# Queue order of the weight sums in the first 58 steps, another ring for one factor of the rotation table, and moved slots in a hybrid decoder layer

## The chip, the cores and the metric

The kernel runs on one core of one Trainium2 chip. The metric is the device time of one execution in microseconds (us): 2327.57 us is the median of three runs (2327.4 to 2328.82). The profile shows one further execution of the same program.

## The reference, cut to what matters

One decoder layer for 512 tokens of width 2048, in float32:

```python
h = rms_norm(x, g_mix)
aq, ak, av, rq, rk, rv, rg = split(h @ w_in)          # 7 parts of 1024 columns
# 8 attention heads: QK-RMSNorm, rotation, block-sparse causal softmax attention
# 8 retention heads: rotation, decayed q k^T v in chunks, per-head RMS norm, silu(rg) gate
x = x + concat(a_out, r_out) @ w_o                    # w_o 2048 x 2048
h2 = rms_norm(x, g_ffn)
x = x + (silu(h2 @ w_gate) * (h2 @ w_up)) @ w_down    # 5632 wide
gate = sigmoid(rms_norm(x, g_ple) @ w_ple_gate + b_ple_gate)
x = x + (p @ w_ple_proj) * gate
```

The rotation multiplies with tables of cosines and sines. The retention heads use a transposed table `ropeT` of 128 x 2 x 512 values; in this kernel it is first multiplied by the inverse norm of each token's row, because `h` here is only scaled by the gain and not yet by the norm.

## The kernel before, in words

**Products.** Every float32 operand is split in a high and a low part (`split`, L51: ScalarE copies the high part, `wh` for weights; VectorE subtracts it from the source, which gives the low part `wl`). A product is three matmuls (`mm3`, L72): high with high, high with low, low with high. The large products use a Strassen-like scheme: of 2 x 2 blocks seven products are made, named "1", "5", "6", "3", "7", "2", "4" in this order. "5", "6", "7" and "4" need a sum of two weight blocks. VectorE makes it in place (`Group.add`, L317, which calls `plus` at L83, shown as `raw<-raw`), and then the sum is split.

**Steps.** `run` (L173) works through a list of steps, each one product name with one unit of 256 rows of weights. In iteration `i` it first calls `before(i)`, then adds for step i+3, extracts (splits) for step i+2 and multiplies for step i. In the iterations named by `close` the add is for step i+2. The loop only writes the program order. A planner then orders each engine's instructions by priority and by the times that it reckons with, so an instruction can run earlier than where it stands. `tc.issue_after(ins)` binds the instructions in its block to stand behind `ins` in the queue of that engine. Matmuls keep the program order (`in_order`). A group of four units has 28 steps. The last call of `run` (L1395) has 2 groups of the output product (`w_ow`), 11 of gate and up, 6 of down and 2 of the last gate; its adds are bound only behind `last_p`, which is the last multiplication of the last retention head.

**The stage between.** From about 350 to 700 us attention and retention are interleaved with five projections of `h` (`projection`, L781). Each projection has 32 slots of six matmuls into four banks `acc`. `at_slot(n, fn)` puts a piece of other work into slot n, `tick` (L735) runs it. The tables `V_AT`, `T3`, `ATTEND`, `RETAIN` and `MIXED` (L1136 to L1145) hold the slots: turning q and k (`turned`), scores, turning the softmax weights (`weights_turned`), the head's result, and `mixed`, which splits two heads' results into the seven factors of the output product. `in_place` (L909) rotates an attention block, `qk_ret` (L1005) takes a retention projection from its banks: ScalarE copies the halves crosswise (`mr`, L1015 and L1016), VectorE multiplies the bank by the table (`zr`, L1017), and only then is the bank free for the next projection; later `turned` (L1019) multiplies `mr` by the other half of the table and adds it.

**Rings.** Tiles of one tag share a few buffers. The ring "A" has two; a head's result stays in it until `mixed` has read it. The ring "rm" has four; `m`, `sq`, `mr` and some outputs of `mixed` use it. `tp` has two banks for transposes.

**The table.** `load_ropeT` (L838) stands in slot 58: a DMA of the table, four transposes that spread the inverse norm over the partitions, a ScalarE copy of these to `bc` (in ring "A"), and a VectorE product.

**The banks of the output product.** `multiply` (L352) of the first group, for product "1", takes four banks in one go, in the order X0, Z0, Z1, X1; they take the places of the four `acc` banks, whose last content (`pp`) ScalarE copies out at L1212. `take_over` (L1224) runs the last 16 slots inside the first eight iterations of the last `run`.

Of the kernel before, what the change touches and what calls it, by code (L numbers as in the profile page):

```python
# [33 lines left out]
def layer_kernel(ctx, tc, x, xT, pT, g_mix, wqk, w_vg, qk_norm, g_ret, w_ow, g_ffn,  # L34
# [135 lines left out]
    def later(n, fn):  # L170
        due.setdefault(now[0] + n, []).append(fn)

    def run(before=lambda i: None, behind=False, close=()):  # L173


        i = -3
        parts = {}
        while i < len(steps) or due:
            now[0] = i
            before(i)  # L180
            todo = [(2, "extract"), (3, "add"), (0, "multiply")]
            if i in close:
                todo = [(2, "add"), (2, "extract"), (0, "multiply")]
                if i + 1 not in close:
                    todo[2:2] = [(3, "add")]
            for n, act in todo:
                if 0 <= i + n < len(steps):
                    g, p, u = steps[i + n]
                    with ExitStack() as queued:
                        if act == "add" and (not behind or i < 8) and i not in close and parts.get(i + 1):  # L190
                            queued.enter_context(tc.issue_after(parts[i + 1][1].ins))
                        if act == "add" and last_p:
                            queued.enter_context(tc.issue_after(last_p[-1].ins))
                        made = getattr(g, act)(p, u)
                    if act == "extract":
                        parts[i + n] = made
                        splits.append(made)
            with ExitStack() as queued:
                for ins in parts.pop(i + 1, ()) if behind else ():
                    queued.enter_context(tc.issue_after(ins.ins))  # L200
                for fn in due.pop(i, []):
                    fn()
            i += 1
        steps.clear()

    def ev_tile(tag, bufs=2, shape=(P, T), name=None, dt=F32):
        return pools["ev"].tile(list(shape), dt, name=name or tag, tag=tag, bufs=bufs)
# [77 lines left out]
    class Group:  # L285
# [66 lines left out]
        def multiply(self, p, u):  # L352
            wh, wl = self.w.pop((p, u))
            k = BANK[p]
            first = p in OPENS and self.left[p] == len(self.units)
            if first:
                def bank(k, b):
                    return pools.get("chain" + k, pools["chain"]).tile([P, T], F32, name=k + str(b), tag=k + str(b))
                if self.spread and p == "1":
                    x = bank("X", 0)  # L360
                    self.bank["Z"] = [bank("Z", 0), bank("Z", 1)]
                    self.bank["X"] = [x, bank("X", 1)]
                elif not (self.spread and p == "5"):
                    self.bank[k] = [bank(k, b) for b in range(2)]
            self.left[p] -= 1
            last = self.left[p] == 0
            self.w[u] = wh, wl
            whole, lo, hi = (0, T), (0, T // 2), (T // 2, T)
            todo = [(0, u, whole), (1, u, whole)]
            if self.ends and p == "4":  # L370
                todo = [(0, u, whole)]
                if first:
                    self.bank["H"] = pools["chain"].tile([P, T], F32, name="Z1", tag="Z1")
                for c in (lo, hi) if self.left[p] != 1 else ():
                    todo += [(1, v, c) for v in ((u - 1, u) if last else (u,))]
            in_order[0] = in_order[0] or self.ends and p == "4"
            for b, v, (c0, c1) in todo:
                at = slice(b * P, (b + 1) * P)
                to = self.bank["H"] if c0 else self.bank[k][b]
                for c in range(2):  # L380
                    s = self.tiles[p].pair(2 * v + c)
                    mm3(to[:, :c1 - c0], s[:, 0, at], s[:, 1, at], *(x[:, c, c0:c1] for x in self.w[v]),
                        first and c == 0, last and v == u and c == 1, p in "237")
            if last:
                self.after(p)
                self.evac(self, p)
# [344 lines left out]
    def at_slot(n, fn):  # L731
        assert n > slot[0]
        pieces.setdefault(n, []).append(fn)
# [104 lines left out]
    def load_ropeT():  # L838
        t = ap.tile([P, 2, T], F32, name="ropeT", tag="rope")
        nc.sync.dma_start(t, ropeT_c)  # L840
        bc = ev_tile("A", name="bc")
        nc.scalar.activation(bc, over_partitions(rstd1), AF.Copy)
        nc.vector.tensor_tensor(t, t, bc[:, None, :].to_broadcast([P, 2, T]), op=ALU.mult)
        tables.append(t)
# [78 lines left out]
    def qk_attn(i):  # L923

        made, norms = [], []
        if i == 0:
            for b in range(NB):
                with tc.issue_after(splits[b - 5][1].ins):
                    in_place(0, b, made, norms)
        elif i < NPAIR - 1:  # L930
            for b in range(NB):
                at_slot((2 + b, 15 + b)[i - 1], lambda b=b: load_block(i, b, lead[0]))
                at_slot(((7, 11, 17, 20), (24, 30, 33, 36))[i - 1][b], lambda b=b: in_place(i, b, made, norms))
        else:
            zs = []
            for acc in projection(True):
                zs.append(rp_tile("z"))
                nc.scalar.activation(zs[-1], acc, AF.Copy)
            blocks[i] = zs
            for b in range(NB):  # L940
                def go(b=b):
                    known.setdefault(i, {})[b] = ms = stat.tile([P, 4], F32, name="ms", tag="rsqk", bufs=NB)
                    with behind_weights():
                        squares_of(zs[b], ms, b, rm_tile("sq"))
                    in_place(i, b, made, norms)
                at_slot(T3[b], go)
        return made, norms
# [57 lines left out]
    def qk_ret(i):  # L1005
# [25 lines left out]
                made[f] = parted(got[f][0])  # L1031
        for f, (z, m) in enumerate(got):
            if i < 2 * NPAIR - 1:
                at_slot(slot[0] + (6 + 2 * f if i < 2 * NPAIR - 2 else 7 + f), lambda z=z, m=m: turned(z, m))
                made.append(z)
        return made

# [87 lines left out]
    def mixed(i, made):  # L1125
# [3 lines left out]
        with ExitStack() as queued:  # L1129
            for ins in lead if i < 2 * NPAIR - 1 else ():  # L1130
# [1 line left out]
            factors(*made, lambda p: (direct if p in s_o else spilled)(p))  # L1132

    four = lambda n, m=None: (n, n + 1, *((n + 4, n + 5) if m is None else (m, m + 1)))
    V_AT = (3, 31, 55, 82, 108, 124, 145, 162)
    T3 = (48, 50, 52, 56)  # L1136
    ATTEND = (((4, four(7, 10), (11, 12, 14, 15), 20), (12, four(16, 21), four(21), 30)),
              ((23, four(26, 31), four(31, 38), 44), (34, four(39, 45), four(45), 53)),
              ((48, four(53), four(57), 70), (59, four(63, 73), four(72, 77), 81)),
              ((75, four(79), four(83), 92), (85, four(89), four(93, 103), 107)))  # L1140
    RETAIN = (((104, 103, 108, 114, 118, 121), (112, 105, 116, 122, 126, 128)),
# [3 lines left out]
    MIXED = (37, 67, 83, 109, 139, 152, 170, 192)  # L1145

    def heads(i, made):

# [9 lines left out]
        if i < NPAIR:  # L1158
            for j, (turns, steps_s, steps_w, last) in enumerate(ATTEND[i]):
                turned, scores, weights_turned, result = attend(*made, v, j)  # L1160
                put(turned, turns, turns + 1)
                put(weights_turned, *steps_w)
                put(scores, *steps_s)
                end(last, result)
        else:
            for j, (first, at, step_s, step_n, step_x, last) in enumerate(RETAIN[i - NPAIR]):
                begin, load, load_gate, scores, normed, scaled, result = retain(made, v, j, 2 * (i - NPAIR) + j)
                if (i, j) == (2 * NPAIR - 1, 1):
                    plan.append((170, load_gate))
                plan.extend(((first, begin), (at, load), (step_x, scaled)))  # L1170
                put(scores, *range(step_s, step_s + NB))
                put(normed, step_n, step_n + 1)
                end(last, result)
        for n, fn in plan:
            at_slot(n, fn)
# [2 lines left out]
    at_slot(2, lambda: nc.scalar.activation(stat.tile([P, 1], F32, name="sm"), neghalf, AF.Exp))  # L1178
    for i in range(2 * NPAIR):
        if i == NPAIR:  # L1180
            at_slot(58, load_ropeT)
        qk = qk_attn(i) if i < NPAIR else qk_ret(i)
        heads(i, qk)
    assert not gu_moves
# [207 lines left out]
        if i == b_at:  # L1392
            load_bias()

    run(before, True, range(-3, 10))  # L1395


def _constants():
# [68 lines left out]
```

## Time and profile before

| what | value |
|---|---|
| median of three runs | 2327.57 us |
| the profiled execution: its own time | 2327.24 us |
| its span (first to last instruction) | 2325.2 us |
| TensorE matmul busy | 2292.1 us, 99% |
| VectorE busy | 1917.9 us, 82% |
| ScalarE busy | 1243.3 us, 53% |
| GpSimd busy | 103.6 us, 4% |
| mean granted TensorE clock | 0.996 |

The execution's own time is 2.0 us more than its span, and 0.3 us less than the median. In the rows, PE is the TensorE's matmuls, PEld its weight loads, DVE is VectorE, ACT ScalarE, POOL GpSimd and SPq the queue that issues most DMAs. A time in square brackets behind a row is the engine's idle time just before it, with the instruction that ended it.

### The profile page before, as it was taken

The page shows a single profiled execution, that of the slowest core. Times are in us where ns is not written, and L with a number is a line of the kernel's source. Part 1 is how long each engine was busy: PE and PEld are TensorE (multiplying, and loading weights), DVE is VectorE, ACT ScalarE, POOL GpSimd, SP SyncE. Part 2 cuts the span into 40 slices and gives each one's busy share as a digit, 9 for nine tenths or more (in the row PEclk, how much of TensorE's full clock was granted, in tenths as well). Part 3 has the DMA queues.
Part 4 walks back from the last instruction along what each step waited for, and adds up shares of the span by engine and source line. Part 5 has one row for each costly group of instructions (what it writes and reads, how often), then busy time and mean ns, then how long its engine had stood idle before and what let it go on. Part 6 is the DMA issues. An engine that isn't in the chain of part 4 may idle for free.

```text
span 2325.2 us, 29619 instructions
## 1 busy us (share of the span) xinstructions
PE 2292.1 (99%) x10445; PEld 1893.7 (81%) x10445; DVE 1917.9 (82%) x2569; ACT 1243.3 (53%) x1975; POOL 103.6 (4%) x135
## 2 busy tenths in 40 slices
PE   9999999989998999999999999999999999999999
PEld 7888887868887878888888888888888888888877
DVE  8877888767677987888988898889888887788798
ACT  8645555545675566545554555455445443447643
POOL 0002000100120000000000000000000000000000
PEclk9999999999999999999999999999999999999999
DMA  6736845546686789467546754775596776869863
GB/s 238 244 141 202 276 155 170 180 125 196 181 289 254 279 283 375 140 215 252 162 149 224 247 157 156 229 233 154 189 392 200 257 294 205 299 233 357 292 205 127
DMA packets 184133, 520.78 MB, mean 224 GB/s; under 512 B 20273, under 2 KB 33201, under 8 KB 179761
## 3 DMA queue, kind: packets, MB, share of 16 engines
q1 hardware_dynamic: 169888, 468.54, 56.3%
q0 software_dynamic: 13952, 50.34, 10.0%
q8 instruction: 82, 1.34, 0.2%
q14 instruction: 67, 0.54, 0.1%
q10 hardware_dynamic: 144, 0.01, 0.0%
HBM read 415.00 MB, written 149.95 MB: 243 GB/s over the span
## 4 chain that ended last, share of the span: by engine, by line
PE 67%; DVE 4%; DMA 2%; issue 1%; ACT 1%; SPq 0%; DVEq 0%; ACTq 0%
PE Y L63 27%; PE Z L63 17%; PE X L63 17%; PE acc L63 4%; PE tp L68 2%; DVE raw L83 1%; DVE wl L55 1%; PE at L63 1%; DMA h<-o 1%; ACT wh L54 1%; DMA raw<-in_w_ow 0%; DMA raw<-in_w_dn 0%; DMA pp<-pp 0%; DVE o L55 0%; DVE t L80 0%
## 5 line engine op out<-in xcount | busy, mean ns | idle before, releaser
L54 ACT ACTIVATE wh<-raw 128x1024 fp32r<-128x1024 f32 (+1 forms) x740 | 783.0, 1059 | 863.6 <-PE Y L63 330.6
L55 DVE TENSOR_TENSOR wl<-raw,wh 128x1024 fp32r<-128x1024 f32 (+1 forms) x740 | 900.4, 1219 | 302.2 <-ACT wh L54 297.8
L63 PE MATMUL Y<-wh,s 128*128 128x512 f32 (+1 forms) x1704 | 537.5, 389 | 1.0 <-ACT wh L54 1.0
L83 DVE TENSOR_TENSOR raw<-raw 128x1024 f32<-128x1024 f32 x348 | 419.1, 1216 | 11.6 <-DMA raw<-in_w_dn 7.2
L63 PE MATMUL Z<-wh,s 128*128 128x512 f32 x1212 | 383.0, 390 | 0.0
L63 PEld LDWEIGHTS Y<-wh,s 128*128 128x128 f32 x1704 | 319.2, 188 | 67.0 <-ACT wh L54 1.8
L63 PE MATMUL Y<-wl,s 128*128 128x512 f32 x852 | 332.5, 390 | 0.0
L63 PE MATMUL X<-wh,s 128*128 128x512 f32 x1008 | 318.3, 389 | 1.4 <-ACT pp L1212 1.4
L63 PEld LDWEIGHTS Z<-wh,s 128*128 128x128 f32 x1212 | 227.8, 188 | 46.3
L63 PE MATMUL Z<-wl,s 128*128 128x512 f32 (+1 forms) x606 | 238.8, 394 | 5.7 <-DVE wl L55 5.7
L63 PEld LDWEIGHTS X<-wh,s 128*128 128x128 f32 x1008 | 189.3, 188 | 40.7 <-ACT pp L1212 1.6
L63 PE MATMUL X<-wl,s 128*128 128x512 f32 x504 | 197.0, 391 | 0.4 <-DVE wl L55 0.4
L63 PEld LDWEIGHTS Y<-wl,s 128*128 128x128 f32 x852 | 160.0, 188 | 33.0 <-DVE wl L55 0.3
L63 PE MATMUL acc<-h,wh 128*128 128x512 f32 x512 | 164.7, 403 | 7.5 <-DVE zr L1017 7.5
L63 PE MATMUL Y<-wh,r 128*128 128x512 f32 x520 | 170.8, 390 | 1.3 <-ACT wh L54 1.1
L63 PEld LDWEIGHTS Z<-wl,s 128*128 128x128 f32 x606 | 114.2, 188 | 30.5 <-DVE wl L55 7.4
L63 PE MATMUL Z<-wh,r 128*128 128x512 f32 x372 | 121.8, 388 | 0.0
L63 PEld LDWEIGHTS Y<-wh,r 128*128 128x128 f32 x520 | 97.4, 188 | 21.8 <-ACT wh L54 2.1
L63 PEld LDWEIGHTS acc<-h,wh 128*128 128x128 f32 x512 | 93.2, 192 | 24.1 <-issue 7.4
L63 PEld LDWEIGHTS X<-wl,s 128*128 128x128 f32 x504 | 94.6, 188 | 20.6 <-DVE wl L55 1.3
L63 PE MATMUL Y<-wl,r 128*128 128x512 f32 x260 | 102.3, 393 | 0.5 <-DVE wl L55 0.5
L63 PE MATMUL acc<-h,wl 128*128 128x512 f32 x256 | 101.5, 396 | 0.0
(246 smaller groups left out, 2821.7 us busy)
## 6 DMA issues: line engine op xcount, KB each, us to landing
raw<-in_w_gu SPq DMA_DIRECT2D x172, 512.0 KB, 5.6
raw<-in_w_dn SPq DMA_DIRECT2D x85, 512.0 KB, 6.4
a<-o SPq DMA_DIRECT2D x154, 256.0 KB, 4.9
raw<-in_w_vg SPq DMA_DIRECT2D x64, 512.0 KB, 5.7
s<-a SPq DMA_DIRECT2D x21, 1536.0 KB, 8.7
raw<-in_wqk SPq DMA_DIRECT2D x47, 512.0 KB, 4.7
raw<-in_w_ow SPq DMA_DIRECT2D x32, 512.0 KB, 7.3
xin<-x SPq DMA_DIRECT2D x60, 256.0 KB, 5.9
```

What stands on the lines that cost most here:

```text
L54: return (nc.scalar.activation(H, src, AF.Copy), nc.vector.tensor_tensor(L, src, H.bitcast(F32), op=ALU.subtract))
L55: nc.vector.tensor_tensor(L, src, H.bitcast(F32), op=ALU.subtract))
L63: ins = nc.tensor.matmul(*args, **kw)
L68: ins = nc.tensor.transpose(o, a, ident)
L83: nc.vector.tensor_tensor(o, a, b, op=ALU.add)
```

## The change

1. `run` gets an argument `kept_back`. An add for a step that it names is queued behind the low part (`wl`) of the step two before it. The last `run` is called with `range(58)`: the two groups of the output product and the first two steps of the next group, which adds nothing on VectorE.
2. `bc`, the factor of the rotation table, comes from ring "rm" instead of ring "A", and `load_ropeT` stands in slot 61 instead of 58.
3. In the first group of the output product the bank Z0 is taken ahead of X0.
4. Slots move. The tables are written out in full, but only these numbers differ: the load of v for the second pair from 31 to 34; the second rotation in place of the second pair from 11 to 13; for the first head `turned` from 4 and 5 to 3 and 4; for the first head of the third pair `turned` from 48 and 49 to 47 and 48, scores from 53, 54, 57, 58 to one later, `weights_turned` from 57, 58, 61, 62 to one later, its result from 70 to 71; in the retention, one `begin` from 120 to 116, three of the four scores of one head from 146 on to one later, `scaled` of that head from 155 to 159 and its result from 158 to 160, one result from 184 to 185, a load of a gate from 170 to 171; the third rotation of the first retention projection from 74 to 78 and of the third from 137 to 134.

```diff
-    def run(before=lambda i: None, behind=False, close=()):
+    def run(before=lambda i: None, behind=False, close=(), kept_back=()):
...
-        parts = {}
+        parts, lows = {}, {}
...
+                        if act == "add" and i + n in kept_back and i + n - 2 in lows:
+                            queued.enter_context(tc.issue_after(lows[i + n - 2].ins))
...
                         parts[i + n] = made
+                        lows[i + n] = made[1] if made else None
...
                 if self.spread and p == "1":
+                    z = bank("Z", 0)
                     x = bank("X", 0)
-                    self.bank["Z"] = [bank("Z", 0), bank("Z", 1)]
+                    self.bank["Z"] = [z, bank("Z", 1)]
...
-        bc = ev_tile("A", name="bc")
+        bc = rm_tile("bc")
...
-                at_slot((2 + b, 15 + b)[i - 1], lambda b=b: load_block(i, b, lead[0]))
-                at_slot(((7, 11, 17, 20), (24, 30, 33, 36))[i - 1][b], lambda b=b: in_place(i, b, made, norms))
+                at_slot(Z_LOAD[i - 1][b], lambda b=b: load_block(i, b, lead[0]))
+                at_slot(Z_AT[i - 1][b], lambda b=b: in_place(i, b, made, norms))
...
-                at_slot(slot[0] + (6 + 2 * f if i < 2 * NPAIR - 2 else 7 + f), lambda z=z, m=m: turned(z, m))
+                at_slot(R_TURN[i - NPAIR][f], lambda z=z, m=m: turned(z, m))
...
-                    plan.append((170, load_gate))
+                    plan.append((171, load_gate))
...
-            at_slot(58, load_ropeT)
+            at_slot(61, load_ropeT)
...
-    run(before, True, range(-3, 10))
+    run(before, True, range(-3, 10), range(58))
```

More of the change, by code (lines that the diff above doesn't have):

```diff
@@ L1134, in layer_kernel @@
     four = lambda n, m=None: (n, n + 1, *((n + 4, n + 5) if m is None else (m, m + 1)))
-    V_AT = (3, 31, 55, 82, 108, 124, 145, 162)
+    V_AT = (3, 34, 55, 82, 108, 124, 145, 162)
     T3 = (48, 50, 52, 56)
[L1137 to L1141, printed above, removed]
[3 rows of a table removed]
+    Z_AT = ((7, 13, 17, 20), (24, 30, 33, 36))
+    Z_LOAD = ((2, 3, 4, 5), (15, 16, 17, 18))
+    ATTEND = (((3, (7, 8, 10, 11), (11, 12, 14, 15), 20),
[7 rows of a table added]
+    RETAIN = (((104, 103, (108, 109, 110, 111), (114, 115), 118, 121),
[7 rows of a table added]
     MIXED = (37, 67, 83, 109, 139, 152, 170, 192)
+    R_TURN = ((70, 72, 78, 76), (102, 104, 106, 108), (135, 136, 134, 138))
     def heads(i, made):
@@ L1168, in heads @@
                 if (i, j) == (2 * NPAIR - 1, 1):
-                    plan.append((170, load_gate))
+                    plan.append((171, load_gate))
                 plan.extend(((first, begin), (at, load), (step_x, scaled)))
-                put(scores, *range(step_s, step_s + NB))
-                put(normed, step_n, step_n + 1)
+                put(scores, *step_s)
+                put(normed, *step_n)
                 end(last, result)
```

17 rows, old and new, of tables (ATTEND, RETAIN) are left out of this document.

## The prediction

> **What bounds the kernel.** I read the page first, then TensorE's waits, then windows around the longest, then the rows in order of time.
>
> ```profile
> span 2325.2 us, 29619 instructions
> PE 2292.1 (99%) x10445; PEld 1893.7 (81%) x10445; DVE 1917.9 (82%) x2569; ACT 1243.3 (53%) x1975; POOL 103.6 (4%) x135
> ```
>
> TensorE is busy for all but 33.1 us of the span, and the change removes no matmul. It can gain only from what TensorE waits for, and from the clock that it is granted behind a wait. The waits, with the engine's line, who ended them, us in total, times and the longest:
>
> ```profile
> PE acc L63 <- DVE zr L1017: 7.5, 2, 7.0
> PE Z L63 <- DVE wl L55: 5.7, 3, 4.8
> PE tp L68 <- DVE PL L55: 3.5, 3, 2.6
> PE Y L63 <- ACT wh L54: 2.1, 3, 1.1
> PE tp L68 <- DVE pt L977: 2.1, 2, 1.8
> PE tp L68 <- DVE qkL L55: 0.6, 1, 0.6
> PE at L63 <- DVE PL L55: 0.4, 1, 0.4
> ```
>
> Three waits make over half of it. Windows of the three and of the stretch behind each; the columns are the window and its length, busy us (and instructions) of PE, PEld, DVE, ACT and POOL, the granted clock, the DMA share, and GB/s:
>
> ```profile
> 446.87:449.50 2.63, 0.01 (x1) 0.01 (x1) 2.63 (x8) 2.56 (x14) 0.43 (x1) 0.95 0.32 73
> 449.26:452.67 3.41, 3.17 (x10) 2.69 (x11) 3.41 (x8) 1.38 (x5) 2.62 (x2) 0.50 0.30 115
> 480.94:487.95 7.01, 0.00 (x0) 0.03 (x1) 6.11 (x14) 4.49 (x10) 0.00 (x0) 0.67 0.50 145
> 487.95:493.63 5.68, 5.68 (x13) 4.43 (x14) 1.65 (x3) 0.00 (x0) 0.00 (x0) 0.50 0.27 102
> 720.66:725.50 4.84, 0.00 (x1) 0.00 (x0) 4.84 (x6) 2.05 (x5) 0.00 (x0) 1.00 0.13 48
> 725.74:729.15 3.41, 3.41 (x9) 2.62 (x9) 3.12 (x3) 0.00 (x0) 0.00 (x0) 0.50 0.00 0
> ```
>
> Behind each of the three the clock is 0.50, for 3.41, 5.68 and 3.41 us. Matmuls that run 3.17, 5.68 and 3.41 us at half speed lose half of that: 1.6, 2.8 and 1.7 us. So the waits cost 4.2, 9.8 and 6.5 us. VectorE has work during nearly all of each: its order is the matter, not its amount.
>
> **The table's factor (edit 2).** The wait of 7.0 us in order of time:
>
> ```profile
> 460.22 0.61 SPq L840 DMA_DIRECT2D ropeT<-in_ropeT_c  x1
> 466.82 0.62 PE L68 MATMUL tp<-ident,rstd 128*128 128x128 f32 x4
> 484.22 0.60 ACT L842 ACTIVATE bc<-tp 128x512 f32<-128x512 f32 x1 [0.35 <-DVE t L80]
> 484.98 1.22 DVE L843 TENSOR_TENSOR ropeT<-ropeT,bc 128x1024 f32<-128x1024 f32 x1
> 487.12 2.48 DVE L1017 TENSOR_TENSOR zr<-acc,ropeT 128x512 f32<-128x512 f32 x4
> DMA to landing us min/median/max: 6.6/6.6/6.6
> ```
>
> The table had landed at 466.8 and the four transposes were done at 467.4. The copy `bc` came 16.8 us later, released by `t`, a subtraction of `mixed`: ring "A" holds two heads' results, and `mixed` frees one. Ring "rm" is not held so: its `m` of the last rotation in place is read before the table's slot, and `mr` is written only after it. A slot has six matmuls of 0.23 us (200 us for 884, in a row further down), so slot 61, the fourth from the end of its projection, begins at 480.94 - 4 x 1.36 = 475.5 at the latest. Transposes (0.62 us), copy (0.60) and product (1.22) end by 477.9, ahead of 480.94 when the first bank is wanted. The instructions stay the same, one DMA, four transposes, one copy, one product, and ScalarE and VectorE have room there: in the wait itself VectorE was idle for 0.9 us and ScalarE for 2.5. The first row of waits holds one more change of projections, at 0.5 us; I leave that here too: 7.0 - 0.5 + 2.8 = 9.3 us. The ends are 9.8 and, if the DMA comes late, a loss (first rival). The copy also held one of the two `tp` banks for 17 us. The row of `PL` above has 0.9 us in two short waits besides the long one; with both banks in use I take 0.5 of these (ends 0 and 0.9).
>
> **Turning the first head of the third pair one slot earlier (edit 4).** The wait of 2.6 us:
>
> ```profile
> 444.54 0.49 PE L68 MATMUL tp<-ident,pt 128*128 128x128 f32 x3
> 447.31 0.48 ACT L54 ACTIVATE PH<-tp 128x384 fp32r<-128x384 f32 x1
> 448.89 0.55 DVE L55 TENSOR_TENSOR PL<-tp,PH 128x384 fp32r<-128x384 f32 x1
> 449.50 1.11 PE L68 MATMUL tp<-ident,pt 128*128 128x128 f32 x4 [2.63 <-DVE PL L55]
> ```
>
> The transposes of 444.54 (slot 49) keep their bank until VectorE has read it at 449.4; right behind them, in the same slot, `turned` takes the other, and slot 50 needs the first again. With `turned` in slots 47 and 48, slot 50 takes the bank of slot 48 instead, which is read a slot's 1.4 us earlier or more. The moved work, eight transposes and two splits, is the same. Of 4.2 us I take 3.5, as a wait of some 0.5 to 0.7 can stay where ScalarE and VectorE were busy 2.56 and 2.63 of 2.63 us; the ends are 0 and 4.2.
>
> [...]
>
> **The adds behind the low parts (edit 1).** The wait of 4.8 us:
>
> ```profile
> 716.48 0.69 DVE L1098 TENSOR_TENSOR r<-r,sg 128x512 f32<-128x512 f32 x1
> 717.09 4.62 DVE L83 TENSOR_TENSOR raw<-raw 128x1024 f32<-128x1024 f32 x4
> 718.34 2.26 ACT L54 ACTIVATE wh<-raw 128x1024 fp32r<-128x1024 f32 x2 [1.76 <-DVE raw L83]
> 721.97 2.35 DVE L83 TENSOR_TENSOR raw<-raw 128x1024 f32<-128x1024 f32 x2
> 724.24 3.48 DVE L55 TENSOR_TENSOR wl<-raw,wh 128x1024 fp32r<-128x1024 f32 x3
> 725.50 0.62 PE L63 MATMUL Z<-wl,s 128*128 128x512 f32 x1 [4.84 <-DVE wl L55]
> ```
>
> The adds wait for the last head's `r<-r,sg`, then six run in a row. The first one's high part is ready at 719.4, but its low part starts at 724.24, behind five adds that nobody needs yet. With the edit, the third add has to stand behind that low part: add to 718.3, the second add to 719.4, the low part to 720.7. TensorE stops at 720.66, so some 0.3 us of waiting stays. The five adds then come one at a time between low parts, in time in which TensorE no longer stands still; for this I leave 0.5 us more (the two short waits of the same row are 0.9 together). 6.5 - 0.8 = 5.7 us; ends 0.8 (all given back, second rival) and 6.5. The edit issues nothing new and adds no DMA; in VectorE's queue everything behind a low part that waits for its `wh` now waits too, adds among it.
>
> **The banks (edit 3).**
>
> ```profile
> 702.65 0.58 ACT L1212 ACTIVATE pp<-acc 128x512 f32<-128x512 f32 x1
> 703.28 0.50 PE L63 MATMUL X<-wh,s 128*128 128x512 f32 x1 [1.37 <-ACT pp L1212]
> ```
>
> X0 sits in the bank that is copied out last. If Z0 takes that place, it is wanted only after X's three steps, and X0 and X1 have banks copied before: 1.4 us, with ends 0 (another order of banks) and 1.4. I take 1.3.
>
> **The other slots.** The wait for `pt` (1.8 us):
>
> ```profile
> 508.62 1.29 DVE L1024 TENSOR_TENSOR mr<-mr,ropeT 128x512 f32<-128x512 f32 x2
> 510.48 1.28 DVE L1025 TENSOR_TENSOR zr<-zr,mr 128x512 f32<-128x512 f32 x2
> 514.21 0.52 PE L68 MATMUL tp<-ident,pt 128*128 128x128 f32 x3 [1.80 <-DVE pt L977]
> ```
>
> Two rotations, 2.6 us of VectorE, lie just ahead of it. One moves from slot 74 to 78, so half, 1.3 us, goes; I take 1.2 (ends 0 and 2.1, that row's total). `turned` of the first head and the second rotation in place lie near the wait for `qkL`, 0.6 us: half, 0.3 (ends 0 and 0.6). The rest (the load of v, four DMAs, and of a gate, one DMA, later in SP's queue; `begin`, two splits; three scores; `scaled`, four ScalarE copies; three results; the rotation from 137 to 134) moves by one to four slots where the only waits listed are the 0.4 us for `PL` and parts of short ones; I take 0, bounds 0.4 either way.
>
> **Sum.** 9.3 + 0.5 + 3.5 + 5.7 + 1.3 + 1.2 + 0.3 = 21.8 us. New short waits will come where the order is new: I allow three of 0.4 us, the size of the short ones of `Z`, 1.2. That leaves 20.6. The profiled execution takes 2327.24 (its span and 2.0 us around it), so 2306.6; the median of the runs lies 0.3 above it: 2306.9.
>
> **The rivals.** (1) The table is late by its DMA. Slot 61 lies behind fetches of weights in SP's queue:
>
> ```profile
> 466.04 17.38 SPq L758 DMA_DIRECT2D raw<-in_wqk  x3
> ```
>
> Behind the third of them it would be issued at 483.4, land 6.6 us later at 490.0, and free the first bank at 492, some 4 us later than now: instead of 9.3 gained 4 lost, 2320. For it: the queue is in order. Against: the table was issued at 460.22, seven us ahead of its slot's transposes, as soon as its buffer was free, and behind the first fetch alone it would still land by 473. Chance 0.10.
>
> (2) The adds' gain is given back: the low parts and adds that ran during the stall pile up on VectorE in the steps behind. 2306.9 + 5.7 = 2312.6. For and against it stand these rows:
>
> ```profile
> 100.00:300.00 200.00, 200.00 (x884) 165.68 (x883) 163.56 (x170) 107.38 (x198) 22.88 (x26) 1.00 0.62 203
> 760.00:850.00 90.00, 89.54 (x409) 73.54 (x408) 85.29 (x112) 53.05 (x87) 0.00 (x0) 1.00 0.73 255
> DVE wl L55 <- ACT wh L54: 297.8, 305, 7.6
> ```
>
> For it: from 760 to 850 VectorE is 95% busy. Against: its 4.7 us of idle time there could still take up most of what piles up. Chance 0.13.
>
> (3) Slower: VectorE becomes the bound of the output product. Each of the 32 adds (four of its seven products, four units, two groups) now stands behind a low part that waits for ScalarE, 297.8 / 305 = 0.98 us on average, and that idling was filled by adds. 32 x 0.98 = 31.4 us against 90 - 85.3 = 4.7 us of idle time: TensorE is 26.7 us late, and the 5.7 of the edit don't come: 2339. It begins to tell once the new idling exceeds 4.7 us, and it outweighs the other gains (20.6 - 5.7 = 14.9 us) above 19.6. Against it: from 100 to 300 us the same rule already holds for the adds of the first `run` (its other binding, behind the low part of step i+1), and TensorE doesn't wait at all there with VectorE at 82%. Chance 0.08.
>
> (4) The change doesn't do what it says, as slots are only priorities to the planner, and the stalls reappear a few us on: 2327. Chance 0.06.
>
> **How the numbers follow.** The forecast has 0.63. What a measurement of this kernel can tell from no change is about 0.2%, 4.7 us. Faster by more: the forecast, (1) and (2), 0.86; within it: (4), 0.06; slower: (3), 0.08. If every term comes at its better end (9.8 + 0.9 + 4.2 + 6.5 + 1.4 + 2.1 + 0.6 = 25.5) and the short waits of `Z` and `Y` go too (0.9 + 2.1), the time is 2299; the upper end, 2321, takes in (2) and (1). Beyond these lie (3) and (4).
>
> **What would show it.** The copy `bc` within 3 us of its transposes and no wait of `acc` above 0.6 us near 480; no wait of 2 us for `PL` near 448; at about 715 a low part behind the second add, and the row of `Z` waiting for `wl` below 1.5 us; no wait for `pp`; the granted clock 1.00 in all three places. Wrong: a DMA as what ends the wait of `ropeT`, VectorE idle for `wh` ahead of adds from 760 to 850 with waits of X, Y or Z, or new windows at 0.50.

## The result, and the profile after

The changed kernel takes 2297.79 us (median of 2297.44 to 2298.71), the kernel before 2328.07 beside it: ratio 0.987, interval 0.9853 to 0.9888. The forecast was 2306.9 us with a range from 2299.0 to 2321.0. The direction was right, the gain of 30.3 us is half as large again as the 20.6 forecast, and the time lies 1.2 us below the range. All executions used below are fast ones, except one of 3650.89 us at a granted clock of 0.587 in the run with `turned` alone in its old slots, which is left out of that run's figures.

The head of the page of the profile, and the longest of TensorE's waits (engine, line, who ended them; us in total, times, longest):

```profile
span 2295.6 us, 29635 instructions
PE 2283.2 (99%) x10445; PEld 1890.5 (82%) x10445; DVE 1917.4 (84%) x2569; ACT 1242.5 (54%) x1975; POOL 102.5 (4%) x135
```

```profile
PE Y L63 <- ACT wh L54: 2.3, 2, 1.1
PE tp L534 <- DVE zeros L529: 1.2, 1, 1.2
PE tp L68 <- DVE PL L55: 0.9, 1, 0.9
PE Z L63 <- DVE wl L55: 0.8, 2, 0.4
PE acc L63 <- DVE zr L1021: 0.5, 1, 0.5
```

The three long waits are gone and the granted clock is 1.00 where it was 0.50. Windows around the three old places (window and length; busy us of PE, PEld, DVE, ACT, POOL; clock, DMA share, GB/s):

```profile
445.50:450.20 4.70, 4.70 (x26) 3.88 (x24) 4.38 (x11) 4.13 (x19) 0.94 (x1) 1.00 0.31 76
473.70:481.90 8.20, 8.20 (x39) 6.77 (x38) 7.32 (x21) 6.78 (x14) 0.00 (x0) 1.00 0.57 174
693.30:705.40 12.10, 12.10 (x59) 9.70 (x57) 10.44 (x12) 7.63 (x18) 1.44 (x1) 1.00 0.70 279
```

TensorE is idle for 2295.6 - 2283.2 = 12.4 us of the span, 20.7 less than before; and it is busy 8.9 us less with the same 10445 matmuls. Of the 8.9, 6.1 are the half clock behind the three waits (1.6 + 2.8 + 1.7). The other 2.8 us are neither idle time nor clock: by subtraction, and as my estimate, they are waiting that the profile counts as busy matmuls. In the starts below they sit mostly where the waits sit.

Since the order of the large matmuls is nearly the same, the start of the same one can be compared in the two traces. Slots are counted by the six `acc` matmuls of each, steps by twelve matmuls of the output product; us from the span's start:

| place | before | after | gained so far | in this stretch | forecast |
|---|---|---|---|---|---|
| slot 1 | 355.3 | 356.1 | -0.8 | -0.8 | 0 |
| slot 49 | 445.2 | 445.5 | -0.3 | 0.5 | 0.3 |
| slot 52 (past the wait for `PL`) | 454.2 | 450.2 | 4.1 | 4.4 | 3.5 |
| slot 62 | 475.8 | 469.7 | 6.1 | 2.0 | 0.5 |
| slot 69 (past the late table) | 496.2 | 480.5 | 15.6 | 9.5 | 9.3 |
| slot 81 (past the wait for `pt`) | 523.7 | 504.9 | 18.8 | 3.2 | 1.2 |
| first step of the output product | 703.3 | 682.4 | 20.9 | 2.1 | 1.3 |
| sixth step begins | 720.3 | 699.3 | 21.0 | 0.1 | 0 |
| seventh step | 729.7 | 702.3 | 27.4 | 6.4 | 5.7 |
| thirteenth step | 747.8 | 719.1 | 28.7 | 1.3 | 0 |
| 59th step | 880.8 | 850.2 | 30.6 | 1.9 | 0 |
| end of the matmuls | 2319.7 | 2290.1 | 29.6 | -1.0 | 0 |

The forecast column adds to 21.8, and 1.2 were taken off for new waits.

The table's factor in order of time, in the kernel after:

```profile
456.17 0.60 SPq L844 DMA_DIRECT2D ropeT<-in_ropeT_c  x1
467.64 0.60 PE L68 MATMUL tp<-ident,rstd 128*128 128x128 f32 x4
468.65 0.59 ACT L846 ACTIVATE bc<-tp 128x512 f32<-128x512 f32 x1
469.93 1.22 DVE L847 TENSOR_TENSOR ropeT<-ropeT,bc 128x1024 f32<-128x1024 f32 x1
471.88 0.68 DVE L1021 TENSOR_TENSOR zr<-acc,ropeT 128x512 f32<-128x512 f32 x1
```

The copy starts 0.4 us behind the transposes, where it had been 16.8, and the first bank is being read at 471.9, ahead of 475.1, when slot 65 wants it. The DMA of the first rival is still issued early, 11 us ahead of the transposes.

VectorE at the start of the output product, after:

```profile
695.29 0.69 DVE L1102 TENSOR_TENSOR r<-r,sg 128x512 f32<-128x512 f32 x1
695.90 2.35 DVE L83 TENSOR_TENSOR raw<-raw 128x1024 f32<-128x1024 f32 x2
698.37 1.22 DVE L55 TENSOR_TENSOR wl<-raw,wh 128x1024 fp32r<-128x1024 f32 x1
699.52 1.22 DVE L83 TENSOR_TENSOR raw<-raw 128x1024 f32<-128x1024 f32 x1
700.99 1.22 DVE L55 TENSOR_TENSOR wl<-raw,wh 128x1024 fp32r<-128x1024 f32 x1
```

Two adds, then the low part, then add and low part in turn: the order of the forecast. The low part ends at 699.6 while the sixth step begins at 699.3, and no wait stands there in the list.

### The profile page after: what moved, and what is told of

Same layout as the page of the kernel before. It is cut to its first block, busy times and chain, and to the rows that moved or that the text cites. A ratio compares the mean times of both kernels' runs of the same rounds, so it can differ in the third digit from the quotient of the medians.

```text
span 2295.6 us, 29635 instructions
## 1 busy us (share of the span) xinstructions
PE 2283.2 (99%) x10445; PEld 1890.5 (82%) x10445; DVE 1917.4 (84%) x2569; ACT 1242.5 (54%) x1975; POOL 102.5 (4%) x135
## 4 chain that ended last, share of the span: by engine, by line
PE 70%; DVE 2%; DMA 2%; issue 1%; ACT 0%; SPq 0%; ACTq 0%; DVEq 0%
PE Y L63 27%; PE Z L63 19%; PE X L63 17%; PE acc L63 5%; PE tp L68 2%; PE at L63 2%; DVE raw L83 1%; DVE wl L55 1%; DMA raw<-in_w_dn 1%; DMA xin<-x 1%; DMA s<-a 0%; DMA pp<-pp 0%; DMA x<-xin 0%; ACT wh L54 0%; DVE e L83 0%
```

## The experiments

Theory 1 through all of them: each edit removes the waits of its own place. Its rival: the planner orders everything anew, so the gain is a joint one, and undoing a part shows little or something else. Each run stands beside the kernel before on the same chip, and the ratios are to that.

**The adds unbound.**

```diff
-    run(before, True, range(-3, 10), range(58))
+    run(before, True, range(-3, 10))
```

> The changed kernel with its adds of the last run bound as in the kernel before. Theory 1 (each edit removes the waits of its own place): the wait of 4.8 us for a low part in the sixth step of the output product is back, with 3.4 us at clock 0.50 behind it, and most of the short waits up to step 55: 6.5 to 9.5 us, 2304 to 2307. Theory 2 (the planner orders the whole stage anew, and the other edits alone already break up the row of adds): within 1 us of the changed kernel, 2297 to 2299, and no wait above 1 us there.

Measured: 2307.5 us, ratio 0.9908 (0.9891 to 0.9924). In the matmuls' starts the difference to the changed kernel is 0 up to the sixth step, 5.8 at the seventh, 7.2 at the thirteenth, 7.6 at the 59th. VectorE and TensorE there:

```profile
695.84 6.90 DVE L83 TENSOR_TENSOR raw<-raw 128x1024 f32<-128x1024 f32 x6
702.65 1.21 DVE L55 TENSOR_TENSOR wl<-raw,wh 128x1024 fp32r<-128x1024 f32 x1
```

```profile
703.92 0.50 PE L63 MATMUL Z<-wl,s 128*128 128x512 f32 x1 [4.33 <-DVE wl L55]
```

The six adds run in a row again, and the wait is back. Theory 1 holds, at the upper end.

**The binding alone, in the kernel before.** The lines of `kept_back` and nothing else.

> The kernel before with the adds bound behind the low part two steps back, nothing else. Theory 1 (the binding removes the long wait and the short ones up to step 55): 9.3 us faster than before, ratio 0.996. Theory 2 (it removes the long wait alone; the short ones of steps 32 to 55 come from elsewhere): 6.4 to 7.7 us faster, ratio 0.9967 to 0.9973. Theory 3 (given back later, the second rival): below 2 us.

Measured: 2319.5 us, ratio 0.996 (0.9945 to 0.9975). The matmuls' starts gain 6.1 between the sixth and the seventh step, 1.3 to the thirteenth, and 1.9 more to the 59th: theory 1. (The interval of the ratio holds theory 2 too; the 9.3 us of the starts decide.) Added to the kernel before, then, the binding also removes the short waits down to the end of the output product, which I had not counted.

**The factor back in ring "A".**

```diff
-        bc = rm_tile("bc")
+        bc = ev_tile("A", name="bc")
```

> The changed kernel with the table's factor back in ring A (slot 61 kept). Theory 1: the copy of the factor waits for mixed again, some 12 us or more behind its transposes; the first bank of the next projection comes 7 us late, half clock behind it, and a short wait or two for the held transpose bank: 9.9 to 11.6 us, 2307.7 to 2309.4. Theory 2 (the slot and the other moved slots carry the gain, not the ring): below 2 us, 2298 to 2300.

Measured: 2310.07 us, ratio 0.9916 (0.9901 to 0.9931). The copy and the wait:

```profile
479.54 0.60 ACT L846 ACTIVATE bc<-tp 128x512 f32<-128x512 f32 x1 [0.35 <-DVE t L80]
```

```profile
PE acc L63 <- DVE zr L1021: 7.7, 2, 7.2
PE tp L68 <- DVE pt L981: 0.5, 1, 0.5
```

The starts lose 11.0 from slot 62 to slot 69 and 0.8 more to slot 81. The second row is new: part of the wait for `pt` in slot 77 is an echo of the late table.

**The ring alone, in the kernel before (slot 58), and the changed kernel with slot 58.**

```diff
-        bc = ev_tile("A", name="bc")
+        bc = rm_tile("bc")
```

> The kernel before with one word changed: the table's factor from ring rm, slot 58 kept. Theory 1 (the ring carries the table's gain, its slot nothing): 11 to 13 us faster than before, ratio 0.994 to 0.9953, the copy within 3 us of its transposes. Theory 2 (the slot is needed too): the copy is early, but another wait of 2 us or more stands near slots 58 to 64, and the gain is below 8 us.

Measured: 2316.55 us, ratio 0.9951 (0.9934 to 0.9967): theory 1. The starts gain 1.4 between slots 57 and 62 (the transpose bank), 10.0 to slot 69, and 1.5 to slot 81. In this trace 1.4 more at slot 50 are the clock, 1.00 behind the same wait (below); 1.7 are lost near 2248 us, and the mean granted clock is 0.998.

```diff
-            at_slot(61, load_ropeT)
+            at_slot(58, load_ropeT)
```

> The changed kernel with the table's load back in slot 58, the ring stays rm. Theory 1 (the ring alone carries the gain): within 0.5 us, the copy some 6 us earlier than in slot 61. Theory 2 (the slot spares a transpose bank or ScalarE in a full stretch): a wait of tp of 0.5 to 2 us near 460 to 466.

Measured: 2298.83 us in two executions, ratio 0.9877 (0.9858 to 0.9897), against 0.987 for the changed kernel; from slot 1 to the 59th step the starts keep the same distance within 0.1 us. The ring carries the gain, the slot nothing.

**X0 ahead of Z0.**

```diff
-                    z = bank("Z", 0)
                     x = bank("X", 0)
-                    self.bank["Z"] = [z, bank("Z", 1)]
+                    self.bank["Z"] = [bank("Z", 0), bank("Z", 1)]
```

> The changed kernel with X0 taken ahead of Z0 again. Theory 1: X's first matmul waits 1.4 us for the last copy of pp again, nothing else: 2299.2. Theory 2: the 1.4 us are hidden by the chain from the last head to the first bound add, so that the sixth step starts no later: 2297.8, within 0.4 us.

Measured: 2299.24 us, ratio 0.9871 (0.9856 to 0.9886). The whole time can't tell it from the changed kernel, the trace can: the starts lose 1.5 at the first step, by this row, and nothing of it is made up behind.

```profile
PE X L63 <- ACT pp L1226: 1.4, 1, 1.4
```

**The old slots, all of them, then two by themselves.** The table's load stays in slot 61.

```diff
-              ((47, (54, 55, 58, 59), (58, 59, 62, 63), 71),
+              ((48, (53, 54, 57, 58), (57, 58, 61, 62), 70),
...
-    R_TURN = ((70, 72, 78, 76), ...
+    R_TURN = ((70, 72, 74, 76), ...
```

> The changed kernel with the slots of the kernel before (the table's load stays in slot 61). Theory 1: the wait of 2.6 us for PL in slot 50 with half clock behind it (4.3), and the one for pt in slot 77 (2 to 3) are back: 6 to 8 us, 2304 to 2306. Theory 2: the wait in slot 77 was an echo of the late table, and only slot 50 comes back: 4 to 4.5 us, 2302.

> The changed kernel with the first head of the third pair in its slots of before (turned 48 and 49, scores from 53, weights from 57, result 70), all else changed. Theory 1 (this move alone removes the wait in slot 50): the wait of 2.6 us is back, 2.8 us with the clock at 1.00 behind it and up to 4.4 with it at 0.50: 2300.6 to 2302.2. Theory 2 (other moved slots share in it): below 1 us, 2298.8.

> The changed kernel with the third rotation of the first retention projection back in slot 74 (from 78). Theory 1 (VectorE's 1.3 us ahead of the softmax weights make the wait in slot 77): waits for pt near 495 us of 1.3 to 1.8 us together, 2299.2 to 2299.6. Theory 2 (the wait in slot 77 was an echo of the late table): within 0.4 us, 2298.

All old slots: 2305.58 us, ratio 0.9897 (0.9882 to 0.9912). That this lies in the range of theory 1 is in part chance: the wait in slot 50 is back without the half clock, and 2.3 us of the starts are lost behind 1400 us, far from the moved slots, with a mean granted clock of 0.999 against 1.000 in the changed kernel. The first line of the diff alone: 2303.75 us in the median of three executions, 1.5 above the range of theory 1 (the profiled one 2302.18), ratio 0.9894 (0.9877 to 0.991). The second line alone: 2299.8 us, ratio 0.9879 (0.9864 to 0.9894). Among TensorE's waits with all old slots:

```profile
PE tp L68 <- DVE PL L55: 2.8, 2, 2.6
PE tp L68 <- DVE pt L981: 1.3, 2, 0.7
PE tp L68 <- DVE qkL L55: 0.6, 1, 0.6
PE at L63 <- DVE PL L55: 0.4, 1, 0.4
```

and among those with the third rotation alone in slot 74:

```profile
PE tp L68 <- DVE pt L981: 1.3, 2, 0.7
```

The move of `turned` alone removes the wait in slot 50, worth 4.3 us of starts in one trace and 2.8 in another (the clock, below). The move of the third rotation alone removes 1.7 us near slot 77. Of the 3.2 us gained there, then, 1.7 are the rotation's and 0.8 to 1.5 the table's; theory 2's pure echo falls, and theory 1 alone is not the whole either.

**The third rival made stronger: adds one step back.**

```diff
-                        if act == "add" and i + n in kept_back and i + n - 2 in lows:
-                            queued.enter_context(tc.issue_after(lows[i + n - 2].ins))
+                        if act == "add" and i + n in kept_back and i + n - 1 in lows:
+                            queued.enter_context(tc.issue_after(lows[i + n - 1].ins))
```

> The changed kernel with each add bound behind the low part directly before it (one step back, not two). It doubles what the third rival fears. Theory 1 (VectorE has room enough): within 1.5 us of the changed kernel. Theory 2 (the rival's mechanism is real, and only the two steps hide it): from low part to low part the chain is add, high part, low part, 1.2 + 1.1 + 1.2 us, 3.5 against 2.7 us for a step of matmuls; three weight buffers store two steps, 5.4 us, so rows of four such steps are just covered and rows of eight (products 5 and 6 of the second group, 7 and 4 apart) lose about 1 to 3 us, and the time is 2299 to 2302 with waits of Y and Z for wl. Above 2310 the rival's price would be right in full.

Measured: 2311.8 us, ratio 0.9933 (0.9919 to 0.9948): about 14 us lost, 4.8 of it from the sixth to the thirteenth step and 6.5 in steps 33 to 41. VectorE and ScalarE in the first stretch:

```profile
714.95 1.22 DVE L83 TENSOR_TENSOR raw<-raw 128x1024 f32<-128x1024 f32 x1
717.35 1.22 DVE L55 TENSOR_TENSOR wl<-raw,wh 128x1024 fp32r<-128x1024 f32 x1 [1.18 <-ACT wh L54]
718.61 1.22 DVE L83 TENSOR_TENSOR raw<-raw 128x1024 f32<-128x1024 f32 x1
721.04 2.36 DVE L55 TENSOR_TENSOR wl<-raw,wh 128x1024 fp32r<-128x1024 f32 x2 [1.21 <-ACT wh L54]
```

```profile
716.26 1.06 ACT L54 ACTIVATE wh<-raw 128x1024 fp32r<-128x1024 f32 x1 [3.16 <-DVE raw L83]
719.95 2.01 ACT L54 ACTIVATE wh<-raw 128x1024 fp32r<-128x1024 f32 x2 [2.63 <-DVE raw L83]
```

From add to add it takes 3.7 us, for a step of matmuls 2.7: add, high part, low part in a chain, while each engine waits for the other. The mechanism of the third rival is real, though 14 us is half of the 26.7 us that the prediction gave it, so my mark of 2310 for its full price was set too low. Two steps back, two such chains run interleaved, and no such loss shows in this stage. My 1 to 3 us for one step back was too small: nearly all of the loss is in the two rows of eight steps with adds (products "5" and "6" of each group), of which I had counted one, and the chain takes 3.7 us where I reckoned 3.5. The rows of four lose 1.3 to 1.4 us in each group.

**The binding for the whole last run.**

```diff
-    run(before, True, range(-3, 10), range(58))
+    run(before, True, range(-3, 10), range(10 ** 6))
```

> The changed kernel with the binding for all steps of the last run, not the first 58. Theory 1 (an order of adds matters only where they pile up, in the output product): within 1 us. Theory 2 (the bindings also shorten the waits of 0.4 to 1.1 us after 1800 us): 1 to 2.5 us faster. Theory 3 (the third rival, in the stages where VectorE is 87% busy): more than 3 us slower.

Measured: 2307.19 us, ratio 0.9912 (0.9895 to 0.9929), 9 us slower than the changed kernel: theory 3. The starts are equal up to the 59th step and lose 2.6 to 4.3 us at each of three places in the gate and up groups (1276, 1358, 1596 us). At the first, ScalarE and VectorE:

```profile
1274.97 0.42 ACT L54 ACTIVATE o<-A 128x256 fp32r<-128x256 f32 x1 [4.04 <-DMA a<-o]
1275.30 1.04 ACT L54 ACTIVATE wh<-raw 128x1024 fp32r<-128x1024 f32 x1
1278.83 1.06 ACT L54 ACTIVATE wh<-raw 128x1024 fp32r<-128x1024 f32 x1 [1.23 <-DVE raw L83]
```

```profile
1275.42 0.43 DVE L55 TENSOR_TENSOR o<-A,o 128x256 fp32r<-128x256 f32 x1 [2.86 <-ACT o L54]
1276.37 1.23 DVE L55 TENSOR_TENSOR wl<-raw,wh 128x1024 fp32r<-128x1024 f32 x1 [0.52 <-ACT wh L54]
1277.51 1.22 DVE L83 TENSOR_TENSOR raw<-raw 128x1024 f32<-128x1024 f32 x1
```

ScalarE stands 4.0 us behind a store whose buffer it needs, the high part queued behind it comes late, VectorE idles 2.9 us, and the adds that could have filled this idling must stand behind the late low part. With the binding for 58 steps only, they are free there. But the waits for the stores are themselves longer with the binding everywhere. The row of all of them in the changed kernel, then here:

```profile
ACT o L54 <- DMA a<-o: 25.0, 30, 2.1
ACT o L54 <- DMA a<-o: 46.8, 25, 4.6
```

Why, and how much of the 9 us is the lost filling alone, these runs don't separate.

**A further slot.** The change leaves one new wait, 0.9 us in slot 13. The second head's `turned` one slot later:

```diff
-               (12, (16, 17, 21, 22), (21, 22, 25, 26), 30)),
+               (13, (16, 17, 21, 22), (21, 22, 25, 26), 30)),
```

> The changed kernel with turned of the very first pair's second head in slots 13 and 14 (from 12 and 13). It tests the reading of the ring of transpose banks on a wait that the change itself brought, 0.9 us at 377.5: with the move the bank is free in time, and the time to the end of the first projection is 0.6 to 0.9 us shorter; if the reading is wrong, the wait moves to the next transpose and nothing is gained.

Measured: 2300.21 us in two executions, ratio 0.9883 (0.9863 to 0.9903). The wait moved and grew to 1.7 us (now for `qkL`), and the way from slot 1 to slot 17 takes 0.8 us longer. The reading of the transpose banks alone did not do here. No version faster than the changed kernel came out.

## Why the forecast was right in kind and short in size

**What bounds the kernel.** Right: all of the gain is waiting and the clock behind it. (The three long waits are 14.4 us, over half of what the list names, but not of the 33.1 us of idle time.) The failed step is to take a row's total in the list of waits as the most that its edit can gain, from which the range's 2299 came. Two stretches went past that end: 2.0 against 0.9 us for the transpose bank, 3.2 against 2.1 for `pt`. The idle time that went there is only 0.7 and 2.6 us; the rest is of the 2.8 us that stood in matmuls counted as busy.

**The factor.** Right: the ring freed the copy, the bank came in time, the DMA early. 9.3 against 9.5. That the new slot adds nothing the prediction had not said. The term for the transpose bank that the copy held, 0.5, was too small: 2.0 in the stretch, of which the ring alone gives 1.4.

**`turned`.** Right, and the reserve of 0.7 wasn't needed: 4.4. My reading that the clock falls behind 2.63 us of idling was one case of two (below): some 1.5 us of the 4.4 are the clock, which the same wait left at 1.00 in two of five traces.

**The adds.** The long wait went as worked out, 6.4. The failed step is "I leave 0.5 us more" for adds that pile up behind it: the opposite happened. Nothing piled up; the starts gain 1.3 + 1.9 us more down to the 59th step. The runs with the binding undone and alone show 1.4 and 1.3 for the first stretch, which is the binding's, then, and 0.4 and 1.9 for the second. Why the second of these shows only when the binding is added to the kernel before, and hardly when it is taken from the changed one, stays open.

**The banks.** 1.3 against 1.5.

**The other slots.** The failed step is "half, 1.3 us, goes": 3.2 went. The rotation alone is worth 1.7, and the rest, 0.8 to 1.5, belongs to the late table, which I had not seen reach so far.

**The sum.** The 1.2 us for three new waits did not come where I looked for them: one of 0.9 in slot 13, and about a microsecond after 1800 us. Together, measured less forecast: 2.0 (slot 77), 1.5 (transpose bank), 3.2 (steps 7 to 59), 0.9 and 0.7 (reserves for `turned` and for the long wait of the adds), 0.8 (up to the first step), 0.5 in the small rows and the 1.2 are 10.8; 1.8 lost at the start and the end leave the 9.0 us by which 29.6 exceeds 20.6.

**The rivals.** The late DMA didn't come. The gain given back didn't come; its opposite did. The third is shown as a mechanism, about 14 us one step back; in the later stages the binding costs 9 us, where ScalarE also waits longer for stores. The fourth fell: each edit undone brings back the wait of its own place.

## What to carry to other kernels

Where one engine is 99% busy, compare the starts of the same instruction in two traces: here the list of waits left out a tenth of the gain. An order that puts what the bound engine waits for next ahead of work for later removed long and short waits here, but only bound two steps back, so that two chains interleave, and only in the stage where the early work piles up; one step back, or in all stages, the gain is gone again (ratios 0.9933 and 0.9912, against 0.9908 with no binding). Ask of a small one-time tile whose ring it sits in and who empties that ring.

## What the runs showed of the hardware

The same wait of 2.63 us for `PL` stands in five traces. In three of them (the kernel before, `turned` alone put back, and the binding alone) the clock falls to 0.50 for 3.41 us; in two (all old slots, and the ring alone) it stays at 1.00. The wait and the stretch behind it with all old slots, and with `turned` alone:

```profile
447.39:450.02 2.63, 0.00 (x0) 0.00 (x1) 2.63 (x8) 2.57 (x14) 0.43 (x1) 1.00 0.39 61
450.02:453.43 3.41, 3.41 (x17) 2.90 (x18) 3.41 (x7) 1.29 (x3) 2.56 (x2) 1.00 0.28 112
```

```profile
446.62:449.25 2.63, 0.00 (x0) 0.00 (x1) 2.63 (x8) 2.57 (x14) 0.43 (x1) 0.94 0.32 101
449.25:452.37 3.12, 3.12 (x10) 2.64 (x11) 3.12 (x7) 1.15 (x3) 2.33 (x2) 0.50 0.23 88
```

The work in the wait is the same; the cost is 1.5 us apart. What decides between the two, these five traces don't show.

In the kernel before the three stretches at 0.50 begin at 449.26, 483.39 and 725.74 us and last 3.41, 10.24 and 3.41 us; the later two begin 34.13 and 276.48 us behind the first, 10 and 81 times 3.413 us. In the 3.41 us just ahead of them TensorE is idle for 2.40, 2.45 and 3.18 us. If the trace is laid out in steps of 3.413 us from 449.26, the step with the most idle time among the others at 1.00 has 1.70 us, and the clock stays at 1.00 behind it. The three, then that one and the step behind it:

```profile
445.85:449.26 3.41, 1.01 (x5) 0.49 (x3) 3.14 (x8) 3.41 (x19) 0.19 (x1) 1.00 0.21 43
479.98:483.39 3.41, 0.96 (x5) 0.44 (x3) 2.19 (x6) 3.20 (x8) 0.00 (x0) 1.00 0.05 18
722.33:725.74 3.41, 0.23 (x1) 0.24 (x2) 3.41 (x4) 0.38 (x1) 0.00 (x0) 1.00 0.01 5
510.70:514.11 3.41, 1.71 (x9) 1.10 (x7) 3.41 (x9) 2.78 (x6) 0.42 (x1) 1.00 0.25 101
514.11:517.52 3.41, 3.04 (x16) 2.40 (x17) 2.11 (x4) 0.96 (x2) 0.39 (x1) 1.00 0.59 71
```

For an estimate from the 4.3 and 2.8 us above, a wait of this size costs about its length where the clock stays at 1.00, and 1.5 us more where it falls to 0.50 for 3.41 us.
